# Tying a chunk's expert fetches to TensorE's late products, and the last keys' products by token halves

## The chip, the cores and the metric

The kernel runs on one core of one Trainium2 chip. The metric is the time of one execution in device microseconds (us), as the median of several runs. A profile is one further execution with the hardware profiler on, with a time of its own.

## The reference

It is one step of a one-layer decoder trunk (width 1024) on 512 prompt tokens and 32 sample tokens: retention heads beside a convolution module, then a retrieval of experts, each followed by a layer norm. The change lies wholly in the retrieval, which works on each token alone:

```python
idx = e1 * N_KEYS + e2                      # 8 heads x 16 experts of 128*128 per token
gate = softmax(sv)
u = take(peer_u, idx); act = gelu(einsum('phkd,pd->phk', u, xb))
vv = take(peer_v, idx); y = einsum('phk,phkd->pd', gate * act, vv)
x = layer_norm(ALPHA * x + y, ln2_g, ln2_b)
```

Every token has 128 slots (8 heads by 16 experts). An expert's row is 1024 numbers of `peer_u` and 1024 of `peer_v`, all in float32.

## The kernel before

**Two ways to do the same retrieval, side by side.** For 288 of the 544 tokens the kernel *gathers*: for one slot k, one indirect DMA on the GpSimd queue (a *fetch*, `gather`, line 587) brings 128 expert rows of 8 KB, one per token on its partition, 1 MiB in all. VectorE then multiplies the u half with the token and sums it (the *dot*, L590), ScalarE makes the weight from it (L598, L599), VectorE adds the weighted v half to the accumulator (L604). There are three chunks: 128 prompt tokens (indices `I0`, 128 slots), the 32 samples packed four heads side by side (`Is`, 32 slots), and 128 more prompt tokens (`Ib`, 128 slots; the diff tells this second chunk of 128 slots by `len(slots) == 128 and x1 is not x1_0`). The fetched tiles rotate: three buffers of `gp` and, for slots with k % 4 == 3, one of `gx2`. So fetch k starts when slot k-4 has been added up. The instructions of the queue of GpSimd stand in the order of the slots.

For the other 256 tokens the kernel does it *densely* on TensorE, over all 16,384 experts. Experts are taken in 128 groups, called keys here, of 128 experts each. For a key e two things are done, each with a row of 512 KB that SyncE loads into one of the four buffers of `uvp`:

- the *scores* (`scores_of`, L815): eight matmuls of 128x256; ScalarE's Gelu follows (`s_stage`, L915) and VectorE multiplies it with the gate weights (L918);
- the *products* (`v_row` loads, `v_products` multiplies, L924 and L930): for each half b of the tokens (128 each) two matmuls of 128x512 that add into two banks `pB[b][0]` and `pB[b][1]` of PSUM.

The profile shows a float32 matmul as two records, so a key's scores are 16 records and its products 8.

**Stages.** The gate weights of the keys come from one-hot products (`build`, L893 to L906): first those of keys 0 to 95 (`first_keys`), while keys 0 to 7 get their products for half 0 ahead of time. Then `phases` runs:

1. half 1 of keys 4 to 7, whose rows are still loaded, then half 1 of keys 0 to 3, whose rows are loaded again (L972);
2. keys 8 to 31 (L975);
3. keys 32 to 95 (L983). With each of the first sixteen goes a step of `last_keys`, which builds the weights of keys 96 to 127; with each of the next 32 (keys 48 to 79) goes the `s_stage` of one of the keys 96 to 127;
4. keys 96 to 123 (L991), then 124 to 127, written half by half in the text (L995).

`fetched` makes the gathered side: the norm of the first chunk, the sample chunk, its norm (`finish`, L607), then the chunk `Ib` and its norm. `run` interleaves both generators in the text, one step of `phases` and two of `fetched` by turns; the tile framework's scheduler then orders each engine's instructions by its own timeline, keeping data dependencies. `behind` (L166) adds an order without a semaphore. After both, the two halves of the dense tokens get their layer norm straight from the banks (L1024) and are written out.

Of the kernel before, what the change touches and what calls it, by code (L numbers as in the profile page):

```python
# [30 lines left out]
NG2 = NS + 128  # L31
ND = NR - NG2
TB = 8
KX = 48
UV = 4
AHEAD = 8
FREE = 20
EG = (32, 20, 44, 32)
E0S = (0, 32, 52, 96)

# [54 lines left out]
def tile_step(ctx: ExitStack, tc: tile.TileContext, a, o):  # L95
    nc = tc.nc
    V, S, T, G = nc.vector, nc.scalar, nc.tensor, nc.gpsimd
# [17 lines left out]
    def mmps():  # L115
        turn[0] += 1
        return banks[turn[0] % len(banks)].tile([128, 512], F32, name="mm")
# [352 lines left out]
    def residual(bank, xT, blocks, c0):  # L470

        for j, k in enumerate(blocks):
            T.matmul(bank[:, j * 128:(j + 1) * 128], xT[:, k, c0:c0 + 128], scaled, start=(j == 0), stop=False,
                     skip_group_check=True)

    def mix_mm(n, gT, y, c0, wo, xT=None):

        banks_ = [mmps(), mmps()]
        if xT is not None:
            for q in range(2):  # L480
                residual(banks_[q], xT, range(q * 4, q * 4 + 4), c0)
        for src, k0 in ((y, 4), (gT, 0)):
            for q in range(2):
                for s in range(2):
                    for k in range(4):
                        last = T.matmul(banks_[q][:n, s * 256:(s + 1) * 256], src[:, k, c0:c0 + n],  # L486
                                        wo[q * 2 + s][:, k0 + k, :], start=(xT is None and k0 == 4 and s == 0 and k == 0),
                                        stop=(k0 == 0 and s == 1 and k == 3), skip_group_check=True)
        return banks_, last
# [83 lines left out]
        V.reciprocal(sm[:n], sm[:n])  # L573
        V.tensor_mul(gate[:n, e0:e0 + nh], ex[:n], sm[:n].unsqueeze(2).to_broadcast([n, nh, TK]))

    gx2, fence, held = [], [], {}

    def hold(k, ins):

# [2 lines left out]
    def gather(x1, idx, gate, acc, slots):  # L582

        for k in slots:
            spare = gx if x1 is x1_0 and k < KX else (gx2[0] if gx2 and len(slots) == 128 else None)
            t = (spare if spare is not None and k % 4 == 3 else gp).tile([128, 2 * D], F32, name="g")
            G.indirect_dma_start(out=t, out_offset=None, in_=a["uv"],  # L587
                                 in_offset=bass.IndirectOffsetOnAxis(ap=idx[:, k:k + 1], axis=0))
            act = gw.tile([128, 2], F32, name="act")
            dot = V.scalar_tensor_tensor(t[:, :D], t[:, :D], 1.0, x1, op0=OP.mult, op1=OP.mult, accum_out=act[:, 0:1])  # L590
            if x1 is x1_0:
                for k0, ins in held.items():
                    if k >= k0:
                        behind(dot, ins)
            if fence and (len(slots) == 128 or k >= FREE):
                behind(dot, fence[0])
            wgt = gw.tile([128, 1], F32, name="wgt")
            S.activation(act[:, 1:2], act[:, 0:1], AF.Gelu)  # L598
            S.activation(wgt, act[:, 1:2], AF.Copy, scale=gate[:, k:k + 1])  # L599
            v = t[:, D:]  # L600
            if k == slots[0]:
                S.activation(acc, v, AF.Copy, scale=wgt)
            else:
                V.scalar_tensor_tensor(acc, v, wgt, acc, op0=OP.mult, op1=OP.add)  # L604
            yield
# [20 lines left out]
    x1_0 = per.tile([128, D], F32, name="x1_0")  # L626
# [16 lines left out]
    n = NR  # L643
# [34 lines left out]
    pm, last = mix_mm(128, g0, y0, 0, wo)  # L678
# [12 lines left out]
    x1T, xT = xT, xT[:, :, NS:]  # L691
# [103 lines left out]
    ln2 = [bc_row("lng", a["ln2_g"], D), bc_row("lnb", a["ln2_b"], D)]  # L795
    GW = {2: gap.tile([128, EG[2], ND], F32, name="Ga")}

    def place(e):

        g = max(i for i in range(4) if E0S[i] <= e)  # L800
        return GW[g][:, e - E0S[g]]

    def place2(e):

        g = max(i for i in range(4) if E0S[i] <= e)
        return GW[g][:, e - E0S[g]:e - E0S[g] + 2]

    def scores_of(e, ne=1):

        sp = pdn.tile([128, 2, ND], F32, name="sp")  # L810
        for i in range(ne):
            u = uvp.tile([128, D], F32, name="uv").rearrange("p (k e) -> p k e", k=8)
            nc.sync.dma_start(u, a["ut"][e + i])
            for k in range(8):
                T.matmul(sp[:, i], u[:, k], x1T[:, k, NG2:], start=(k == 0), stop=(k == 7), skip_group_check=True)  # L815
        return sp[:, 0:ne] if ne > 1 else sp[:, 0]

    qs = rp.tile([128, 16, n], F32, name="qs")
# [17 lines left out]
    for g in range(2):  # L836
# [9 lines left out]
        p = mmps().rearrange("p (q t) -> p q t", q=4)  # L846
# [16 lines left out]
    gb = gbs.enter_context(tc.tile_pool(name="gb", bufs=1, side="right", reuse_waits="tile"))  # L863
    GW[0] = gb.tile([128, EG[0], ND], F32, name="Gb")
    for e in range(0, EG[0], 2):
        S.activation(place2(e), scores_of(e, 2), AF.Gelu)
# [10 lines left out]
    for b in range(2):  # L877
        for q in range(2):
            residual(pB[b][q], x1T, range(q * 4, q * 4 + 4), NG2 + b * 128)
    GW[1] = gc.tile([128, EG[1], ND], F32, name="Gc")  # L880

# [26 lines left out]
                if t % nt == nt - 1:  # L908
                    yield pt, slice(t - nt + 1, t + 1), mm

    def s_stage(e, n=ND):

        sp, G_ = scores_of(e), place(e)
        W = dw_.tile([128, ND], F32, name="W")
        S.activation(W[:, :n], sp[:, :n], AF.Gelu)  # L915
        if n < ND:
            S.activation(G_[:, n:], sp[:, n:], AF.Gelu)
        V.tensor_mul(G_[:, :n], G_[:, :n], W[:, :n])  # L918

    ahead, marks = [], []  # L920

    def v_row(e):
        vt = uvp.tile([128, D], F32, name="uv")
        nc.sync.dma_start(vt, a["uv"][e * NK:(e + 1) * NK, D:])  # L924
        return vt

    def v_products(e, vt, b):
        W, ps_ = place(e), []
        for q in range(2):
            ps_.append(T.matmul(pB[b][q], W[:, b * 128:(b + 1) * 128], vt[:, q * 512:(q + 1) * 512],  # L930
                                start=False, stop=(e == NK - 1), skip_group_check=True))
        return ps_

    def first_keys():

        with tc.tile_pool(name="bt", bufs=2, reuse_waits="tile") as bt:
            done = 0
            for pt, ts, mm in build(bt, 0, E0S[3], 4):
                for g, e0, e1, ready in ((0, 0, EG[0], True), (2, 0, EG[2], True), (1, 0, done, True), (1, done, EG[1], False)):
                    if e0 == e1:  # L940
# [18 lines left out]
    def last_keys():  # L959

        with tc.tile_pool(name="bt", bufs=2, reuse_waits="tile") as bt:
            for pt, ts, _ in build(bt, E0S[3], EG[3], 16):
                S.activation(GW[3][:, :, ts], pt.rearrange("p t e -> p e t"), AF.Copy)
                yield

    def v_stage(e):
        vt = v_row(e)
        for b in range(2):
            v_products(e, vt, b)

    def phases():
        for e in [*range(AHEAD - UV, AHEAD), *range(AHEAD - UV)]:  # L972
            v_products(e, ahead[e] if e >= AHEAD - UV else v_row(e), 1)
            yield
        for e in range(len(ahead), EG[0]):  # L975
            v_stage(e)
            yield
        gbs.close()
        gd = ctx.enter_context(tc.tile_pool(name="gd", bufs=1, side="right", reuse_waits="tile"))
        GW[3] = gd.tile([128, EG[3], ND], F32, name="Gd")  # L980
        b = last_keys()
        more = iter(range(E0S[3], NK))
        for e in range(E0S[1], E0S[3]):  # L983
            v_stage(e)
            if next(b, "end") == "end":
                for _ in range(1):
                    k = next(more, None)
                    if k is not None:
                        s_stage(k)
            yield  # L990
        for e in range(E0S[3], NK - UV):  # L991
            v_stage(e)
            yield
        ends = [(e, v_row(e)) for e in range(NK - UV, NK)]
        for b in range(2):  # L995
            for e, vt in ends:
                v_products(e, vt, b)
                yield

    def fetched():  # L1000
# [21 lines left out]
    for b in range(2):  # L1022
        t = gp.tile([128, 2 * D], F32, name="g")[:, :D]
# [50 lines left out]
```

## Time and profile before

| | us |
|---|---|
| median of 3 runs (lowest, highest) | 1551.27 (1546.92, 1552.34) |
| the profiled execution's own time | 1557.44 |
| its span, first to last instruction | 1555.7 |
| TensorE busy | 1484.1 |
| VectorE busy | 1227.7 |
| ScalarE busy | 581.4 |
| GpSimd busy | 369.6 |

The mean granted TensorE clock of that execution was 0.983. Times inside the profile are counted from the start of its span. A row of the chain reads: start, duration, engine, tile and line, and how many records. A row of the timeline reads: start, duration, engine, line, operation, output and inputs, count, and in brackets the idle time of the engine just before it with what ended it. A row of the windows has, after the stretch and its length, the busy time of each engine with its number of records, then the granted clock (1.00 is full), the mean busy share of the 16 DMA engines, and the GB/s they moved.

### The profile page before, as it was taken

The page shows a single profiled execution, that of the slowest core. Times are in us where ns is not written, and L with a number is a line of the kernel's source. Part 1 is how long each engine was busy: PE and PEld are TensorE (multiplying, and loading weights), DVE is VectorE, ACT ScalarE, POOL GpSimd, SP SyncE. Part 2 cuts the span into 40 slices and gives each one's busy share as a digit, 9 for nine tenths or more (in the row PEclk, how much of TensorE's full clock was granted, in tenths as well). Part 3 has the DMA queues.
Part 4 walks back from the last instruction along what each step waited for, and adds up shares of the span by engine and source line. Part 5 has one row for each costly group of instructions (what it writes and reads, how often), then busy time and mean ns, then how long its engine had stood idle before and what let it go on. Part 6 is the DMA issues. An engine that isn't in the chain of part 4 may idle for free.

```text
span 1555.7 us, 20736 instructions
## 1 busy us (share of the span) xinstructions
PE 1484.1 (95%) x7046; PEld 1004.1 (65%) x7046; DVE 1227.7 (79%) x3151; ACT 581.4 (37%) x1633; POOL 369.6 (24%) x329
## 2 busy tenths in 40 slices
PE   6999999897999999999999999999999999999997
PEld 6978667565866668788888884444566555543333
DVE  4779998978747999999978988666777777766664
ACT  2224453125112333333534898426992111111110
POOL 2001225322312222312231101222223222322210
PEclk9999999998999999999999999999999999999999
DMA  9648787985688779999999624999999999999993
GB/s 362 243 153 353 252 297 257 347 334 206 226 339 341 273 260 363 358 330 346 366 382 360 240 88 177 394 350 402 347 372 394 423 424 424 424 424 424 424 410 121
DMA packets 100119, 505.85 MB, mean 325 GB/s; under 512 B 10247, under 2 KB 21255, under 8 KB 57125
## 3 DMA queue, kind: packets, MB, share of 16 engines
q0 software_dynamic: 42240, 305.12, 50.4%
q1 hardware_dynamic: 51325, 192.05, 32.4%
q10 hardware_dynamic: 6448, 7.36, 1.5%
q8 instruction: 55, 0.90, 0.2%
q14 instruction: 51, 0.42, 0.1%
HBM read 499.12 MB, written 5.80 MB: 325 GB/s over the span
## 4 chain that ended last, share of the span: by engine, by line
PE 55%; DVE 20%; DMA 12%; issue 9%; POOL 3%; ACT 2%; DVEq 0%; SPq 0%; POOLq 0%; ACTq 0%
PE pB L930 27%; PE sp L815 11%; DMA g<-in_uv_dram,I 6%; PE mm L199 5%; PE mm L486 5%; DVE acc L604 4%; DVE g L590 4%; PE mm L906 3%; POOL g L587 2%; DMA g<-in_uv_dram,Is 2%; DMA g<-in_w_in_dram 2%; DMA uv<-in_uv_dram 1%; PE mm L310 1%; DVE B L901 1%; DVE score L516 1%
## 5 line engine op out<-in xcount | busy, mean ns | idle before, releaser
L815 PE MATMUL sp<-x1T,uv 128*128 128x256 f32 x2048 | 464.1, 383 | 5.2 <-DMA uv<-in_ut_dram 2.8
L604 DVE SCALAR_TENSOR_TENSOR acc<-g,wgt,acc 128x1024 f32<-128x1024 f32 x285 | 364.5, 1279 | 102.0 <-ACT wgt L599 100.4
L815 PEld LDWEIGHTS sp<-x1T,uv 128*128 128x128 f32 x2048 | 384.7, 191 | 78.5 <-issue 28.2
L598 ACT ACTIVATE act<-act 128x1 f32<-128x1 f32 x288 | 57.8, 201 | 625.7 <-DVE g L590 625.4
L587 POOL DMA_INDIRECT g<-in_uv_dram,I x128 | 166.9, 1304 | 460.1 <-DVE acc L604 259.2
L590 DVE SCALAR_TENSOR_TENSOR g<-g,x1g 128x1024 f32<-128x1024 f32 x160 | 195.2, 1222 | 71.8 <-DMA g<-in_uv_dram,Ib 50.5
L587 POOL DMA_INDIRECT g<-in_uv_dram,Ib x128 | 140.6, 1098 | 442.0 <-DVE acc L604 293.7
L199 PE MATMUL mm<-x1T,w 128*128 128x384 f32 (+1 forms) x512 | 178.3, 504 | 1.5 <-ACT score L535 1.2
L590 DVE SCALAR_TENSOR_TENSOR g<-g,x 128x1024 f32<-128x1024 f32 x128 | 154.8, 1214 | 31.0 <-DMA g<-in_uv_dram,I 30.9
L930 PE MATMUL pB<-uv,Ga 128*128 128x512 f32 x352 | 162.1, 604 | 0.2
L893 ACT ACTIVATE off<-row,e1T 128x128 bf16<-128x128 bf16 x512 | 158.0, 388 | 1.0
L199 PEld LDWEIGHTS mm<-x1T,w 128*128 128x128 f32 x512 | 97.4, 192 | 73.7 <-issue 40.3
L930 PE MATMUL pB<-uv,Gb 128*128 128x512 f32 x256 | 113.5, 597 | 4.9 <-DMA uv<-in_uv_dram 4.5
L930 PEld LDWEIGHTS pB<-uv,Ga 128*128 128x128 f32 x352 | 63.7, 189 | 83.4 <-issue 63.1
L930 PE MATMUL pB<-uv,Gd 128*128 128x512 f32 x256 | 115.5, 599 | 0.8
L930 PEld LDWEIGHTS pB<-uv,Gd 128*128 128x128 f32 x256 | 46.7, 190 | 69.7 <-issue 69.5
L930 PEld LDWEIGHTS pB<-uv,Gb 128*128 128x128 f32 x256 | 47.4, 190 | 60.7 <-issue 52.9
L906 PEld LDWEIGHTS <-A 128*128 128x128 bf16 x1536 | 60.5, 96 | 31.3 <-issue 21.3
L901 DVE TENSOR_TENSOR B<-M,gtT 128x768 bf16<-128x768 bf16 (+1 forms) x192 | 69.4, 416 | 9.4 <-PE mm L906 9.2
L930 PE MATMUL pB<-uv,Gc 128*128 128x512 f32 x160 | 72.8, 600 | 0.0
L895 ACT ACTIVATE A<-off 128x1024 bf16<-128x1024 bf16 x64 | 67.4, 1053 | 9.3 <-PE mm L906 8.5
L906 PE MATMUL mm<-B,A 128*128 128x96 bf16 (+1 forms) x1536 | 63.9, 191 | 7.3 <-DVE Gc L947 6.5
(274 smaller groups left out, 1675.4 us busy)
## 6 DMA issues: line engine op xcount, KB each, us to landing
uv<-in_uv_dram SPq DMA_DIRECT2D x132, 512.0 KB
uv<-in_ut_dram SPq DMA_DIRECT2D x128, 512.0 KB
w<-in_w_in_dram SPq DMA_DIRECT2D x18, 1024.0 KB
w<-in_w_query_dram SPq DMA_DIRECT2D x16, 1024.0 KB
w<-in_w_out_dram SPq DMA_DIRECT2D x7, 1024.0 KB
g<-in_uv_dram,I POOLq DMA_INDIRECT x128
keys<-in_state_retention_dram ACTq DMA_DIRECT2D x4, 512.0 KB
out_dram<-keys SPq DMA_DIRECT2D x4, 512.0 KB
```

The costliest lines, as they stand in the source:

```text
L199: T.matmul(p[:, :n], w[m // 2][:, k, (m % 2) * 128:(m % 2 + 1) * 128], xT[:, k, c0:c0 + n], start=(k == 0), stop=(k == 7))
L486: last = T.matmul(banks_[q][:n, s * 256:(s + 1) * 256], src[:, k, c0:c0 + n], wo[q * 2 + s][:, k0 + k, :], start=(xT is None and k0 == 4 a ...
L587: G.indirect_dma_start(out=t, out_offset=None, in_=a["uv"], in_offset=bass.IndirectOffsetOnAxis(ap=idx[:, k:k + 1], axis=0))
L590: dot = V.scalar_tensor_tensor(t[:, :D], t[:, :D], 1.0, x1, op0=OP.mult, op1=OP.mult, accum_out=act[:, 0:1])
L598: S.activation(act[:, 1:2], act[:, 0:1], AF.Gelu)
L604: V.scalar_tensor_tensor(acc, v, wgt, acc, op0=OP.mult, op1=OP.add)
L815: T.matmul(sp[:, i], u[:, k], x1T[:, k, NG2:], start=(k == 0), stop=(k == 7), skip_group_check=True)
L893: S.activation(off[:, t], row, AF.Abs, bias=e1T[:, t1 + t:t1 + t + 1])
L895: S.activation(A, off, AF.Relu, bias=1.0, scale=-1.0)
L901: V.tensor_tensor(B[:, q], M, pairs_of(gtT[:, q], t1).to_broadcast([128, TB // 2, ne, 2]), op=OP.mult)
L906: mm = T.matmul(pt[:, t % nt], A[:, t - t1], B[:, q, (t - t1) // 2, :, t % 2], start=(q == 0), stop=(q == 2))
L930: ps_.append(T.matmul(pB[b][q], W[:, b * 128:(b + 1) * 128], vt[:, q * 512:(q + 1) * 512], start=False, stop=(e == NK - 1), skip_group_che ...
```

## The change

`PACE = (28, 15, 14)`. TensorE's late work is counted in *units*, a list to which matmuls are appended as the program's text comes by: the last matmul of every product pair of keys 48 to 123 and of every score of keys 96 to 127 (in the text: products 48, score 96, products 49, score 97 and so on to products 79, score 127, then products 80 to 123), and, of the last four keys, the last matmul of every second product of a half. That makes 64 + 44 + 4 = 112 units, 0 to 111. Fetch k of the chunk `Ib`, from slot 28 on, gets a semaphore dependency on unit (k - 28) * 15 // 14, so slot 28 waits for unit 0 and slot 127 for unit 106. In the text the generator yields until that unit exists. Fourteen fetches so go with fifteen units.

The first products of `phases` are regrouped: half 1 of keys 4 to 7 as before, then keys 8 to 31, and with keys 8 to 11 the half 1 of keys 0 to 3, one each.

The last four keys' products get an order among TensorE's instructions: those of half 1 stand behind the last one of half 0. In the kernel before, the scheduler had put them key by key, in spite of the text.

```diff
+PACE = (28, 15, 14)
...
+            unit = (k - PACE[0]) * PACE[1] // PACE[2] if len(slots) == 128 and x1 is not x1_0 else -1
+            while unit >= len(units):
+                yield
+            fetch = G.indirect_dma_start(out=t, out_offset=None, in_=a["uv"],
+                                         in_offset=bass.IndirectOffsetOnAxis(ap=idx[:, k:k + 1], axis=0))
+            if unit >= 0:
+                tc.add_manual_dep(fetch.ins, units[unit].ins.name, mybir.DependencyInfo(
+                    mybir.DependencyClass.Sync, mybir.DependencyReason.DATA), reason="pace")
...
-    def scores_of(e, ne=1):
+    def scores_of(e, ne=1, unit=False):
...
+                mm = T.matmul(sp[:, i], u[:, k], x1T[:, k, NG2:], start=(k == 0), stop=(k == 7), skip_group_check=True)
+        if unit:
+            units.append(mm)
...
     def v_stage(e):
         vt = v_row(e)
         for b in range(2):
-            v_products(e, vt, b)
+            ps_ = v_products(e, vt, b)
+        if e >= E0S[1] + ND // 16:
+            units.append(ps_[-1])
...
-        for e in [*range(AHEAD - UV, AHEAD), *range(AHEAD - UV)]:
-            v_products(e, ahead[e] if e >= AHEAD - UV else v_row(e), 1)
+        for e in range(AHEAD - UV, AHEAD):
+            v_products(e, ahead[e], 1)
             yield
-        for e in range(len(ahead), EG[0]):
+        for e in range(AHEAD, EG[0]):
             v_stage(e)
+            if e < 2 * AHEAD - UV:
+                v_products(e - AHEAD, v_row(e - AHEAD), 1)
             yield
...
-                        s_stage(k)
+                        s_stage(k, unit=True)
...
         for b in range(2):
             for e, vt in ends:
-                v_products(e, vt, b)
+                ps_ = v_products(e, vt, b)
+                if b:
+                    for p in ps_:
+                        behind(p, last)
+                else:
+                    last = ps_[-1]
+                if e % 2:
+                    units.append(ps_[-1])
                 yield
```

More of the change, by code (lines that the diff above doesn't have):

```diff
@@ L574, in retrieve @@
         V.tensor_mul(gate[:n, e0:e0 + nh], ex[:n], sm[:n].unsqueeze(2).to_broadcast([n, nh, TK]))
-    gx2, fence, held = [], [], {}
+    gx2, fence, held, units = [], [], {}, []
     def hold(k, ins):
@@ L586, in gather @@
             t = (spare if spare is not None and k % 4 == 3 else gp).tile([128, 2 * D], F32, name="g")
-            G.indirect_dma_start(out=t, out_offset=None, in_=a["uv"],
-                                 in_offset=bass.IndirectOffsetOnAxis(ap=idx[:, k:k + 1], axis=0))
+            unit = (k - PACE[0]) * PACE[1] // PACE[2] if len(slots) == 128 and x1 is not x1_0 else -1
[6 more added lines that the diff above has]
+                    mybir.DependencyClass.Sync, mybir.DependencyReason.DATA), reason="pace")
             act = gw.tile([128, 2], F32, name="act")
@@ L814, in scores_of @@
             for k in range(8):
-                T.matmul(sp[:, i], u[:, k], x1T[:, k, NG2:], start=(k == 0), stop=(k == 7), skip_group_check=True)
+                mm = T.matmul(sp[:, i], u[:, k], x1T[:, k, NG2:], start=(k == 0), stop=(k == 7), skip_group_check=True)
+        if unit:
+            units.append(mm)
         return sp[:, 0:ne] if ne > 1 else sp[:, 0]
@@ L909, in build, with s_stage @@
                     yield pt, slice(t - nt + 1, t + 1), mm
-    def s_stage(e, n=ND):
-        sp, G_ = scores_of(e), place(e)
+    def s_stage(e, n=ND, unit=False):
+        sp, G_ = scores_of(e, 1, unit), place(e)
         W = dw_.tile([128, ND], F32, name="W")
```

## The prediction

> **What bounds the kernel now.** I read the page's slices first, then the windows of the second half, then the chain.
>
> ```profile
> DMA  9648787985688779999999624999999999999993
> 1200.00:1280.00 80.00, 79.11 (x262) 47.70 (x261) 58.51 (x77) 14.78 (x54) 21.28 (x22) 1.00 1.02 424
> 1400.00:1500.00 100.00, 99.21 (x217) 38.81 (x216) 67.00 (x82) 13.44 (x54) 25.28 (x27) 1.00 1.02 424
> 1512.00:1518.00 6.00, 6.00 (x15) 2.48 (x14) 4.10 (x6) 0.62 (x3) 0.00 (x0) 1.00 0.80 301
> 1518.00:1535.00 17.00, 17.00 (x41) 7.50 (x40) 6.72 (x9) 1.95 (x4) 0.00 (x0) 1.00 0.56 186
> ```
>
> From 1200 to 1512 all 16 DMA engines are full (share 1.02, 424 GB/s). Then the fetches are over and the share falls to 0.80 and 0.56, while TensorE still has products to do.
>
> ```profile
> 983.50 79.08 PE pB L930 x184
> ...
> 1130.26 3.53 PE pB L930 x8
> 1134.38 3.55 PE sp L815 x16
> ...
> 1199.18 3.43 PE pB L930 x8
> 1202.62 3.69 PE sp L815 x16
> 1206.31 3.60 PE pB L930 x8
> ...
> 1511.59 33.10 PE pB L930 x76
> ```
>
> The chain runs on TensorE from 983 to 1544.69 (1511.59 + 33.10). A unit is 8 product records or 16 score records, one row of 512 KB. Unstretched, 184 records take 79.08, so a unit takes 8 x 0.43 = **3.44**. Unit 0 starts at 1130.26; scores are the odd units, and the piece at 1202.62 is the tenth of them from 1134.38 on, unit 19. So unit 18 ends at 1202.62. The 93 units from there end at 1544.69; the last 76 records are 9.5 of them, at 3.48. The other 83.5 take 1511.59 - 1202.62 = 308.97, **3.70** each: 0.26 above what TensorE needs.
>
> ```profile
> 1494.08 0.94 POOL L587 DMA_INDIRECT g<-in_uv_dram,Ib  x1 [2.79 <-DVE acc L604]
> 1497.79 0.94 POOL L587 DMA_INDIRECT g<-in_uv_dram,Ib  x1 [2.78 <-DVE acc L604]
> 1505.18 0.94 POOL L587 DMA_INDIRECT g<-in_uv_dram,Ib  x1 [2.75 <-DVE acc L604]
> 1516.61 1.23 DVE L590 SCALAR_TENSOR_TENSOR g<-g,x1g 128x1024 f32<-128x1024 f32 x1 [0.55 <-DMA g<-in_uv_dram,Ib]
> 1518.44 1.29 DVE L604 SCALAR_TENSOR_TENSOR acc<-g,wgt,acc 128x1024 f32<-128x1024 f32 x1 [0.60 <-ACT wgt L599]
> ```
>
> The fetches run at the same step, 3.71. One fetch (1.049 MB) and one row (0.524 MB) in 3.71 us is 1.573 / 3.71 = 0.424 MB per us, just the 424 of the windows. So DMA bounds this stage, TensorE waits 0.26 a unit for its rows, and the last fetch is issued at 1505.18, some 40 us before TensorE ends. It lands 11.43 later, with three others queued ahead of it.
>
> **The change part by part.** *The waits.* No byte and no matmul is added or removed; 100 fetches get one more semaphore.
>
> ```profile
> 1129.63 1.67 POOL L587 DMA_INDIRECT g<-in_uv_dram,Ib  x1 [2.08 <-DVE acc L604]
> ```
>
> This is the 29th fetch of the chunk, slot 28: it starts 4.2 before unit 0 ends (1130.26 + 3.53). At one fetch per unit the fetches now stay ahead; with 14 in 15 units each waits in its turn, more and more of them. A unit's share of DMA is then 0.524 + 14/15 x 1.049 = 1.503 MB; at the 424 GB/s of the windows that takes **3.545**. Bounds: 3.44 below, where TensorE itself is the limit, and 3.683 above, if a unit with a fetch still takes 3.70 and only the fifteenth 3.44. I take 3.545, since the share is 1.02 and TensorE has four row buffers to carry a gain of one unit into the next.
>
> From unit 19 to unit 106 are 88 units: 1202.62 + 88 x 3.545 = **1514.6** for the end of unit 106, at which the last fetch starts (before, unit 106 ended at 1544.69 - 5 x 3.48 = 1527.3).
>
> The Trainium skill, "DMA: Bandwidth & Descriptors", section "Where 436 GB/s comes from", puts transfers from HBM to SBUF at about 358 GB/s; by it a unit would take 4.20 after and 4.39 before, and the windows' 424 speak against it.
>
> Behind a waiting fetch GpSimd has only later fetches. But VectorE and ScalarE work in order too: behind a fetch's dot and its Gelu stand, in the changed order, the one-hot blocks of the last keys that TensorE needs inside units 3 to 9. The tightest: ScalarE's last block stands behind the Gelu of slot 33, which waits for unit 5; TensorE wants it in the middle of unit 9, 3.6 units or about 13 us later. How long a fetch takes on an empty queue the trace shows once, after the pause for the samples' norm (below the window that shows ScalarE full, 39.77 of 40, where those blocks are made):
>
> ```profile
> 1120.00:1160.00 40.00, 40.00 (x324) 25.59 (x323) 29.04 (x64) 39.77 (x118) 11.71 (x9) 1.00 0.97 368
> 1028.29 1.18 POOL L587 DMA_INDIRECT g<-in_uv_dram,Ib  x1 [5.16 <-ACT act L598]
> 1036.45 1.23 DVE L590 SCALAR_TENSOR_TENSOR g<-g,x1g 128x1024 f32<-128x1024 f32 x1 [2.77 <-DMA g<-in_uv_dram,Ib]
> ```
>
> From issue to dot **8.2**; with a full queue 11.4 (above). Dot, Gelu and block add under 3. So 13 is enough at 8.2, and about 1 short at 11.4. A paced fetch meets one other at most: I take 8.2 and cost nothing; the other end is 4 block pairs x 1.
>
> *The last four keys by halves.* Their rows are needed 1.72 apart rather than 3.44. Three rows and a fetch outstanding at unit 106 and one more row at unit 107 are 3.1 MB, 7.4 us at 424 GB/s; the last is wanted 3.44 + 3 x 1.72 = 8.6 after unit 106. Bounds 0 and 5.2 (rows still 3.44 apart); I take 1.0, near the low end. TensorE then ends at 1514.6 + 5 x 3.44 + 1.0 = **1532.8**, 11.9 earlier.
>
> *The tail.* VectorE is in order, and the changed order puts the norm of the gathered chunk in among those of the banks.
>
> ```profile
> 1519.76 1.29 DVE L611 SCALAR_TENSOR_TENSOR yt<-x1g,acc 128x512 f32<-128x512 f32 x2
> 1520.97 1.28 DVE L452 BATCH_NORM_STATS2 lst<-yt 128x6 f32<-128x512 f32 x2
> 1522.53 1.28 DVE L461 SCALAR_TENSOR_TENSOR yt<-yt,lmv,lng 128x1024 f32<-128x1024 f32 x1
> 1524.39 1.28 DVE L466 SCALAR_TENSOR_TENSOR yt<-yt,lrs,lnb 128x1024 f32<-128x1024 f32 x1
> 1544.71 0.70 DVE L452 BATCH_NORM_STATS2 lst<-pB 128x6 f32<-128x512 f32 x1 [0.16 <-PE pB L930]
> 1545.44 0.21 DVE L453 BATCH_NORM_AGGREGATE lmv<-lst 128x2 f32<-128x12 f32 x1
> 1546.18 1.39 DVE L461 SCALAR_TENSOR_TENSOR g<-pB,lmv,lng 128x512 f32<-128x512 f32 x2
> 1551.04 0.15 DVE L464 RECIPROCAL lrs<-lrs 128x1 f32<-128x1 f32 x1
> 1551.22 1.41 DVE L466 SCALAR_TENSOR_TENSOR g<-g,lrs,lnb 128x512 f32<-128x512 f32 x2
> ```
>
> From the last fetch: 8.2 to its dot, 3.1 to the end of its addition (1516.61 to 1519.73), then all the norms in one row: 1.29 + 1.28 + 1.28 + 1.28 for the chunk, per half 1.3 + 0.2 + 1.4 + 0.15 + 1.4, and 0.2 for the chunk's aggregate, 14.2 with its reciprocal, about 14.1 as neighbours overlap. That is 1514.6 + 25.4 = **1540.0**. From TensorE's end: stats 0.7, the chunk's 1.28, half 0's 1.40, stats 0.7, then 0.2 + 1.4 + 0.15 + 1.4 for half 1, less 0.4 as the first stats need not await the last matmul: 1532.8 + 6.8 = 1539.6. The later holds. Before, VectorE ended at 1551.22 + 1.41 = 1552.63 and the span 3.07 later; the output writes stay. So the span becomes 1543.1, **12.6** less than 1555.7.
>
> *The regrouped first products.*
>
> ```profile
> 960.00:1000.00 40.00, 35.51 (x172) 16.55 (x171) 25.95 (x51) 23.25 (x71) 9.38 (x10) 1.00 0.96 371
> 967.00 1.98 PE L930 MATMUL pB<-uv,Gb 128*128 128x512 f32 x4 [1.80 <-DMA uv<-in_uv_dram]
> 971.81 1.98 PE L930 MATMUL pB<-uv,Gb 128*128 128x512 f32 x4 [0.64 <-DMA uv<-in_uv_dram]
> 975.48 1.99 PE L930 MATMUL pB<-uv,Gb 128*128 128x512 f32 x4 [0.97 <-DMA uv<-in_uv_dram]
> 979.21 3.70 PE L930 MATMUL pB<-uv,Gb 128*128 128x512 f32 x8 [1.08 <-DMA uv<-in_uv_dram]
> ```
>
> Here TensorE waits 4.5 in all for rows. The change spreads four half-used rows over four fully used ones, but the same rows have to come and DMA is 0.96 full; and a one-hot block of VectorE now stands behind one fetch more, some 3 to 5 us of possible wait. Between a gain of 4.5 and a loss of 5 I take 0.
>
> **Sum.** The profiled execution would go from 1557.44 to 1544.8. It lies 6.2 above the median shown; the same 12.6 off 1551.27 gives **1539**. About 0.5% (7.8 us) is what a measurement of this kernel can tell from no change: faster means under 1543.5, slower above 1559.
>
> **The rivals.** *Locked to the fetch (0.11).* Rows and fetches go one to one now, 3.70 and 3.71. If that is a turn by turn between the two queues, a unit with a fetch stays 3.70 and the gain is only the fifteenth: 88 x 3.683 puts unit 106 at 1526.7, the span at 1526.7 + 25.4 + 3.07 = 1555.2: **1551**. The Trainium skill, same page, section "Queues, rings and completion order", says that each DMA engine takes turns between its queues, a packet at a time; the equal steps agree. Against it: row buffers fill in the fetchless unit and lend to the next ones.
>
> *The waits never bind (0.05).* If slots stay behind their units, nothing happens: **1551**. Against it: the 4.2 by which slot 28 is early, and 1505.18 for the last.
>
> *TensorE's floor (0.08).* If DMA has more to give, units take 3.44: 88 x 3.44 = 302.7, and with the 4.5 of the first products unit 106 ends at 1500.8, the span at 1529.3, 26.4 less: **1525**. Against it: the share of 1.02 at 424.
>
> *Blocks stuck behind waiting fetches (0.12).* The place is units 3 to 9, where the order leaves 13 us from a unit to the block that stands behind its fetch. From about 10.5 us of landing on, each microsecond more stops TensorE in four block pairs, and paced units hold back the fetches in turn. At 17 it costs 4 x 6.5 = 26 on top of the 12.6 won: **1565**, slower; from 16 it shows. For it: 11.4 with a full queue, and ScalarE full where it happens. Against: 8.2 on an empty one.
>
> **How the numbers follow.** The forecast, 1533 to 1543, gets 0.64; it takes in the row wait and the landing. Faster is 0.64 + 0.08 = 0.72, the same 0.11 + 0.05 = 0.16, slower 0.12. With 0.64 the range must reach the cases at 1551 as well (0.80) and a little of the one below: 1530 to 1553.
>
> **What would show it.** After about 1200: fetch steps of 3.8 rather than 3.71, GpSimd's idle time ended by TensorE, units of 3.55, share still about 1.0, and the fall of the share only in the last 15 us. The last fetch near 1515, issue to dot 8 to 9. In the last 16 product records, half 0's norm work beside half 1. I would be wrong if units stayed at 3.70 with the DMA share below 1, if waits of TensorE for VectorE or ScalarE turned up between 1130 and 1180, or if the last fetch's norm ended over 3 us after 1540.

## The result and the profile after

The changed kernel takes 1551.16 us (median of 22 runs, 1537.03 to 1560.53) beside 1560.04 for the kernel before (22 runs on the same chips, 1546.92 to 1567.5). The ratio is 0.9947, 95% interval 0.9924 to 0.9969: it is faster by 8.3 us, with an interval of 4.8 to 11.9 (the two medians alone lie 8.9 apart). The forecast was 12.6 us off, a ratio of 0.9919, which lies just outside. Two further sets of runs of the same kernel gave 0.9941 (0.9922 to 0.996) and 0.9945 (0.9918 to 0.9972). The forecast time of 1539 missed by 12.2 us, mostly because its base, the median of three runs, was 8.8 below that of 22.

The profiled execution of after took 1559.73 with a span of 1558.0, more than the 1557.44 and 1555.7 of before. The reason shows ahead of the paced part. These two rows are unit 0 (the product behind a batch of small matmuls) and unit 19 in the timeline of TensorE, after:

```profile
1137.77 3.68 PE L939 MATMUL pB<-uv,Gc 128*128 128x512 f32 x8
...
1209.79 3.62 PE L822 MATMUL sp<-x1T,uv 128*128 128x256 f32 x16
```

Unit 0 starts at 1137.77 rather than at 1130.26, and unit 19 at 1209.79 rather than at 1202.62. The 7 us were there before any wait could act. Another profile of the very same kernel starts unit 0 at 1142.88, and one of the variants below at 1126.55, with the same work ahead of it:

```profile
1142.88 3.68 PE L939 MATMUL pB<-uv,Gc 128*128 128x512 f32 x8
```

```profile
1126.55 3.68 PE L939 MATMUL pB<-uv,Gc 128*128 128x512 f32 x8
```

The scatter stands ahead of the regrouped part already: in the profiles of this document the first product of half 1 starts anywhere from 953.5 to 971.2. The granted clock goes some of the way with it (0.97 up to unit 0 in the profile that starts it at 1142.88, 0.98 in the one at 1126.55). So single spans are of no use here for an effect of 8 us. What can be compared is the stretch from unit 0 to VectorE's last instruction: 1552.63 - 1130.26 = 422.4 before. After, the last fetches, and what VectorE does with the last one, are these rows of the timelines of GpSimd and VectorE:

```profile
1517.83 0.94 POOL L591 DMA_INDIRECT g<-in_uv_dram,Ib  x1 [2.78 <-PE pB L939]
1525.21 0.94 POOL L591 DMA_INDIRECT g<-in_uv_dram,Ib  x1 [6.44 <-PE pB L939]
1528.94 0.94 POOL L591 DMA_INDIRECT g<-in_uv_dram,Ib  x1 [2.79 <-PE pB L939]
```

```profile
1538.15 1.23 DVE L597 SCALAR_TENSOR_TENSOR g<-g,x1g 128x1024 f32<-128x1024 f32 x1 [1.84 <-DMA g<-in_uv_dram,Ib]
...
1539.99 1.28 DVE L611 SCALAR_TENSOR_TENSOR acc<-g,wgt,acc 128x1024 f32<-128x1024 f32 x1 [0.60 <-ACT wgt L606]
1541.31 1.29 DVE L618 SCALAR_TENSOR_TENSOR yt<-x1g,acc 128x512 f32<-128x512 f32 x2
...
1553.51 1.41 DVE L467 SCALAR_TENSOR_TENSOR g<-g,lrs,lnb 128x512 f32<-128x512 f32 x2
```

The fetches now stop for TensorE (the releaser in the brackets is a product, L939, where before it was VectorE's addition), one unit is skipped between 1517.83 and 1525.21, and the last fetch starts at 1528.94 rather than 1505.18. VectorE ends at 1554.92, so the stretch is 417.2, 5.2 less than before; in the two further profiles of the change it is 413.4 and 413.3. The mean, 7.8 less, is what the times say.

DMA works longer, until the last fetch has landed at about 1538: the windows of after, with the DMA share and the GB/s as the last two columns:

```profile
1200.00:1280.00 80.00, 79.54 (x271) 50.53 (x270) 55.02 (x73) 13.43 (x52) 23.95 (x22) 1.00 1.01 418
1400.00:1500.00 100.00, 99.46 (x221) 40.08 (x220) 65.22 (x79) 12.93 (x52) 37.28 (x26) 1.00 1.01 417
1512.00:1518.00 6.00, 5.92 (x14) 2.27 (x13) 3.81 (x6) 0.99 (x4) 1.10 (x2) 1.00 1.02 423
1518.00:1535.00 17.00, 16.94 (x40) 7.05 (x38) 10.01 (x12) 1.99 (x8) 2.64 (x3) 1.00 0.99 384
```

From 1518 to 1535 the share is 0.99 instead of 0.56: the emptiness of the old tail is filled. But from 1200 to 1500 it moves 417 to 418 GB/s, not 424. The chain of after (start, duration, engine, tile and line, records), and its first line of shares:

```profile
PE 40%; DVE 24%; DMA 18%; issue 10%; ACT 4%; POOL 3%; SPq 0%; POOLq 0%; DVEq 0%; ACTq 0%
```

```profile
1367.24 11.79 DMA uv<-in_uv_dram
...
1419.77 17.45 PE pB L939 x40
1437.47 11.55 DMA g<-in_uv_dram,Ib
1449.21 11.02 DMA g<-in_uv_dram,Ib
...
1528.94 9.19 DMA g<-in_uv_dram,Ib
```

Before, the chain ran on TensorE from 983 to the end. Now it passes between row loads, TensorE (40 records in 17.45, 3.49 a unit) and fetches, and its end is the last fetch and VectorE's norms behind it, where before TensorE's products led up to the norms.

### The profile page after: what moved, and what is told of

The parts are those of the page before. It is cut to its first block, busy times and chain, and to the rows that moved or that the text cites. A ratio compares the mean times of both kernels' runs of the same rounds, so it can differ in the third digit from the quotient of the medians.

```text
span 1558.0 us, 20737 instructions
## 1 busy us (share of the span) xinstructions
PE 1479.0 (95%) x7046; PEld 1006.9 (65%) x7046; DVE 1226.4 (79%) x3151; ACT 579.5 (37%) x1633; POOL 390.4 (25%) x329
## 4 chain that ended last, share of the span: by engine, by line
PE 40%; DVE 24%; DMA 18%; issue 10%; ACT 4%; POOL 3%; SPq 0%; POOLq 0%; DVEq 0%; ACTq 0%
PE sp L822 13%; PE pB L939 13%; DMA g<-in_uv_dram,Ib 7%; DVE acc L611 6%; PE mm L487 5%; DMA g<-in_uv_dram,I 5%; DVE g L597 4%; PE mm L200 4%; POOL g L591 3%; PE mm L915 2%; DMA uv<-in_ut_dram 2%; DMA g<-in_w_in_dram 2%; ACT off L902 1%; DMA uv<-in_uv_dram 1%; DVE B L910 1%
## 5 line engine op out<-in xcount | busy, mean ns | idle before, releaser
L591 POOL DMA_INDIRECT g<-in_uv_dram,I x128 | 170.7, 1333 | 461.6 <-DVE acc L611 257.9
L591 POOL DMA_INDIRECT g<-in_uv_dram,Ib x128 | 158.7, 1240 | 443.7 <-DVE acc L611 127.7
L939 PE MATMUL pB<-uv,Ga 128*128 128x512 f32 x352 | 159.9, 599 | 1.8 <-DMA uv<-in_uv_dram 1.7
L939 PE MATMUL pB<-uv,Gd 128*128 128x512 f32 x256 | 115.2, 598 | 2.3 <-DMA uv<-in_uv_dram 1.6
L939 PEld LDWEIGHTS pB<-uv,Ga 128*128 128x128 f32 x352 | 65.0, 190 | 80.5 <-issue 64.1
L939 PE MATMUL pB<-uv,Gb 128*128 128x512 f32 x256 | 113.5, 597 | 2.4 <-DMA uv<-in_uv_dram 1.9
L939 PEld LDWEIGHTS pB<-uv,Gd 128*128 128x128 f32 x256 | 46.7, 190 | 70.6 <-issue 62.7
L939 PEld LDWEIGHTS pB<-uv,Gb 128*128 128x128 f32 x256 | 47.3, 190 | 58.0 <-issue 53.0
L939 PE MATMUL pB<-uv,Gc 128*128 128x512 f32 x160 | 72.7, 600 | 0.0
```

The lines of the kernel that those rows point to most:

```text
L591: fetch = G.indirect_dma_start(out=t, out_offset=None, in_=a["uv"], in_offset=bass.IndirectOffsetOnAxis(ap=idx[:, k:k + 1], axis=0))
```

## The experiments

My theory: the whole gain is the spreading of the fetches over more units, and it fell short because units did not get down to 3.545 and the last fetch then sets the end. Rivals: the regrouped first products or the order by halves win or lose something; the waits win by a shorter fetch queue and not by spreading; TensorE, not the fetch, sets the end. All ratios are against the kernel before, run beside the variant on the same chip.

| kernel | ratio (95%) | unit, mean of 18 to 105 | last fetch, from the end of unit 106 | unit 0 to VectorE's end |
|---|---|---|---|---|
| before | 1 | 3.711 | -24.0 | 422.4 |
| the change (three sets) | 0.9947, 0.9941, 0.9945 | 3.621, 3.581, 3.577 | +0.3 | 417.2, 413.4, 413.3 |
| e1 waits only | 0.9943 (0.9913 to 0.9972) | 3.591 | +0.3 | 414.7 |
| e2 all but the waits | 0.9986 (0.9962 to 1.0009) | 3.705 | -29.1 | 421.4 |
| e3 waits and halves | 0.994 (0.991 to 0.997) | 3.603 | +0.3 | 415.5 |
| e4 nine fetches in ten units | 0.9996 (0.9976 to 1.0016) | 3.494 | +18.0 | 419.6 |
| e9 a fetch per unit | 0.9975 (0.9953 to 0.9997) | 3.695 | -21.8 | 418.8 |
| e12 from slot 31 | 0.9941 (0.9921 to 0.9961) | 3.609 | -13.2 | 411.6 |
| e13 from slot 35 | 0.9983 (0.9957 to 1.0009) | 3.697 | -27.1 | 419.9 |
| e5, e17 cap at unit 101 | 0.991 (0.9883 to 0.9938), 0.9951 (0.9931 to 0.9971) | 3.586, 3.571 | -4.0, -2.7 | 412.0, 411.9 |
| e16 cap at 104 | 0.9954 (0.993 to 0.9977) | 3.580 | -4.2 | 411.3 |
| e18 cap at 97 | 0.9948 (0.9928 to 0.9968) | 3.572 | -3.9 | 410.8 |
| e15 waits only, cap at 101 | 0.9968 (0.9945 to 0.999) | 3.586 | -4.5 | 414.2 |
| e10 without the chunk's norm | 0.9916 (0.9889 to 0.9944) | 3.578 | +0.3 | 410.0 |

The last three columns are read from the records of each profile: starts of units 18 and 106, a difference over 88; the last indirect DMA's start; VectorE's last record. (For before, unit 0 is taken where the chain enters it, 0.15 us behind its record.)

**One part alone.** e1 keeps the waits and takes the other two edits back, e3 takes back only the regrouped first products (the first part of the diff), and e2 takes back the waits alone, by a condition that no slot meets:

```diff
-        for e in range(AHEAD - UV, AHEAD):
-            v_products(e, ahead[e], 1)
+        for e in [*range(AHEAD - UV, AHEAD), *range(AHEAD - UV)]:
+            v_products(e, ahead[e] if e >= AHEAD - UV else v_row(e), 1)
...
-                if b:
-                    for p in ps_:
-                        behind(p, last)
```

```diff
-            unit = (k - PACE[0]) * PACE[1] // PACE[2] if len(slots) == 128 and x1 is not x1_0 else -1
+            unit = (k - PACE[0]) * PACE[1] // PACE[2] if False else -1
```

> Only the waits: the order of the first products and that of the last four keys as before. My theory (the spreading of the fetches is the whole gain): the same ratio as the change, about 0.995, units 18 to 106 at 3.62 against 3.71 before, some 8 us less. Rival 'the regrouped first products cost': clearly better than the change, 0.992 or less. Rival 'the halves matter at the end': worse than the change by 2 to 5 us, because the last four rows are then needed by half 0 and half 1 in the old order and the fetch tail stands behind.

> The waits are left out; the regrouped first products and the last keys' new order stay. My theory: no change from the kernel before, 0.998 to 1.002, units back at 3.70 and all fetches over some 35 us before TensorE ends. Rival 'the regroup costs' (in the profile after, 1.0 us came from that stage): 1.001 to 1.004. Rival 'the regroup or the halves are what wins': 0.996 or less.

> Waits and the last keys' new order; the first products as before. My theory: as the change, 0.995, since the regroup is worth between -1 and +1 us. Rival 'the regroup costs': 0.992 or less, and the stretch from the first dense product to key 48 shorter than the change's by several us.

All three came as my theory had it. With the waits alone the ratio is 0.9943; with the waits taken out 0.9986, with an interval that holds 1, and the windows and the chain of e2 are those of before:

```profile
1400.00:1500.00 100.00, 99.08 (x217) 38.67 (x216) 67.96 (x82) 13.43 (x54) 25.36 (x27) 1.00 1.02 424
```

```profile
1494.49 7.34 PE pB L939 x16
1509.32 38.24 PE pB L939 x88
```

Two units take 7.34, 3.67 each, until the fetches are over; then eleven take 38.24, 3.48 each. e3 says that the first products are worth nothing measurable, and the profiles agree: from the first product of half 1 to unit 0 the fourteen with the regrouping take 171.0 to 173.8 us, the four without it 171.9 to 173.4, both 172.3 in the mean. The waits are the cause of the gain: only with them do the units fall from 3.71 to about 3.6.

**Spreading, or a shorter queue?** e9 keeps the waits with one fetch per unit, e4 spreads further, with (28, 10, 9) in the same place:

```diff
-PACE = (28, 15, 14)
+PACE = (28, 1, 1)
```

> One fetch per unit: slot 28 still waits for unit 0, slot 127 for unit 99. The wait is there and the fetches cannot run ahead, but the ratio of fetches to units is that of the kernel before. My theory (only the spreading over more units helps): units at 3.70, unit 18 to 106 at 3.68 to 3.72, ratio 0.998 to 1.002. Rival 'it is the shorter fetch queue that lets rows through': units below 3.62 and a ratio of 0.995.

> Nine fetches in ten units instead of fourteen in fifteen; the last fetch then waits for unit 110 instead of 106. My theory (every skipped fetch frees about nine units to TensorE's floor of 3.44, and the last fetch with the norms behind it sets the end): units near 3.50 to 3.55, so unit 106 some 6 to 9 us earlier than in the change, but the last fetch starts four units (14 us) later in the count, so the span comes out 4 to 8 us longer than the change's, ratio 0.998 to 1.000. Rival 'TensorE's end sets the time': 5 to 8 us faster than the change, 0.990. Rival 'a unit with a fetch is locked at 3.70 whatever the ratio': units 3.67, time some 15 us above the change.

In e9 the units stay at 3.695 and DMA at 424 in the window:

```profile
1400.00:1500.00 100.00, 99.36 (x218) 39.02 (x217) 67.50 (x82) 13.43 (x54) 49.10 (x27) 1.00 1.02 424
```

Its ratio of 0.9975 is a little below what I had put down, but the units are where they were: a wait without fewer fetches per unit shortens nothing there. What its stretch gains, 3.6 us, is mostly the tail: from the end of unit 106 to VectorE's end it takes 21.1 in e9 as in e2, 23.4 before; that is the order by halves. (In e9 only 13 of the 100 fetches start within 0.5 us of their unit's end; the others come up to 3.6 us later, held by DMA's own step of 3.7.) In e4 the units go down to 3.494, the shortest of all, so the spreading is what shortens them. And the time came back all the same. The last fetch in the chain of e4, and VectorE's last record:

```profile
1536.51 5.70 DMA g<-in_uv_dram,Ib
```

```profile
1555.78 2.73 DVE L467 SCALAR_TENSOR_TENSOR g<-g,lrs,lnb 128x512 f32<-128x512 f32 x4
```

The last fetch waits for unit 110 and starts at 1536.51, 18 us after unit 106. Even at 5.70 for the landing, what follows it ends at 1558.51. That is the price of pacing: each unit that the last fetch is put off moves it and all the norms behind it. The forecast for e4, 0.998 to 1.000, held.

**TensorE's own pace.** e11 leaves the fetches of slots 28 to 127 out:

```diff
+            if unit >= 0:
+                yield
+                continue
             fetch = G.indirect_dma_start(out=t, out_offset=None, in_=a["uv"],
```

> Leaves out slots 28 to 127 of the second chunk altogether: their fetches, dots and additions, so that only TensorE's rows are loaded there. Both theories want TensorE's own pace from it: units of 3.44, 303 us from unit 18 to unit 106, about 152 GB/s. If rows alone do not bring the units below 3.5, part of what I put down to the fetches is something else.

One execution took 1534.55. Its chain and one window:

```profile
1361.00 164.81 PE pB L942 x384
```

```profile
1300.00:1400.00 100.00, 100.00 (x306) 57.91 (x305) 3.83 (x9) 3.45 (x9) 0.00 (x0) 1.00 0.47 153
```

384 records in 164.81 are 48 units at 3.43, TensorE's floor. What is above it in the other kernels comes with the fetches; that TensorE then waits for rows, and not for VectorE's work on what was fetched, fits e1 below, where 14 units run at 3.46 with a fetch and its dot for each. And there is something unforeseen in the last two columns: rows alone take 0.47 of the engines' time for 153 GB/s, that is 326 GB/s for a full share, where rows and fetches together reach 424 at 1.02, or 416.

**Why the units did not reach 3.545.** In e1 series of short and of long units follow each other. Its chain and its windows:

```profile
1408.51 48.38 PE pB L939 x112
1464.34 14.18 PE pB L939 x32
1478.54 7.34 PE pB L939 x16
```

```profile
1410.00:1450.00 40.00, 40.00 (x95) 17.68 (x94) 25.63 (x31) 4.98 (x20) 14.90 (x12) 1.00 1.02 418
1465.00:1515.00 50.00, 49.72 (x112) 19.83 (x110) 33.24 (x40) 6.46 (x26) 14.34 (x13) 1.00 1.02 425
```

Behind a skipped fetch 14 units run at 48.38 / 14 = 3.46; behind the next one only three or four do (14.18 for four), and then pairs take 7.34 again, 3.67 each. Over the short units DMA moves 418, over the mostly long ones 425. Four windows of 4 us show one place where it falls, and below them stand the packets of the two queues (q1 has the rows, q0 the fetches; each with packets, MB and its share of the 16 engines' time) from 1227 to 1228:

```profile
1218.00:1222.00 4.00, 4.00 (x17) 2.97 (x16) 2.63 (x5) 0.77 (x3) 1.19 (x1) 1.00 1.02 411
1222.00:1226.00 4.00, 4.00 (x16) 2.57 (x15) 3.40 (x5) 0.50 (x2) 1.19 (x1) 1.00 1.02 425
1226.00:1230.00 4.00, 4.00 (x14) 2.43 (x13) 2.99 (x5) 0.77 (x3) 1.19 (x1) 1.00 0.99 354
1230.00:1234.00 4.00, 4.00 (x18) 3.11 (x17) 3.40 (x5) 0.50 (x2) 1.61 (x2) 1.00 1.01 422
```

```profile
DMA packets 73, 0.28 MB, mean 283 GB/s; under 512 B 10, under 2 KB 10, under 8 KB 67
q1 hardware_dynamic: 63, 0.23, 77.7%
q0 software_dynamic: 10, 0.05, 11.8%
```

From 1226 to 1230 the engines are nearly as busy as ever and move 354; within it, from 1227 to 1228, the rows' queue is nearly alone and 283 GB/s go with a share of 0.90, or 316 for a full one, near the 326 of e11. The packets of the whole stretch say that this is the rule: cut from unit 18 to unit 100 into steps of 1 us, the kernel before has 4% of steps in which the rows' queue takes more than half of the packets' time, the three profiles of the change 12 to 15%. In those steps DMA moves 396 to 404 GB/s in the change; in the steps where the fetches take 50 to 90% of the time it moves 421 to 424, and 424 before. Some 60 to 99% of what the change lacks to 424 falls into those steps (53 to 77% if the steps are made 2 us long, and 36% in e3, so they are not all of it). They are spread over all fifteen units, and not only behind the skipped fetch. Whether the waits leave too little outstanding was tried by counting the slots from a later one, which lets every fetch start some three (e12, the diff) or seven (e13, with 35 for 31) units earlier:

```diff
-PACE = (28, 15, 14)
+PACE = (31, 15, 14)
```

> Fourteen fetches per fifteen units as in the change, but counted from slot 31: every fetch waits for a unit three (here and there four) earlier, the last one for unit 102. What is open is why the paced kernels moved 418 to 421 GB/s from unit 18 to 106 instead of 424. Theory A (a fetch that is bound to the unit just ended leaves DMA too little to do, and three units of slack give it back): units of 3.55 to 3.56, and with the earlier last fetch a ratio of 0.988 to 0.990. Theory B (the paced mixture itself costs it, however loose the wait): units of 3.58 to 3.60, and only the tail is shorter, ratio 0.990 to 0.992 as with the cap. Rival C (so loose a wait binds no more): units above 3.65, ratio 0.995 or more.

> As the last, counted from slot 35: seven or eight units looser, the last fetch waits for unit 98. If the wait still binds in the second half, units lie between 3.55 and 3.65 and TensorE's end sets the time, ratio 0.991 to 0.994: slower than counting from slot 31, because the fetches now end some 10 us before TensorE does and DMA has nothing but rows there. Rival 'earlier is always better for the tail': 0.989 or less.

In e12, theory A fell: 3.609 a unit, and the window moves 421, not 424. (Its waits bind only from about slot 59 on; from unit 48 to unit 106, where they do, a unit takes 3.580 and DMA moves 421 as well.)

```profile
1400.00:1500.00 100.00, 99.67 (x226) 41.36 (x225) 65.93 (x79) 13.05 (x53) 34.67 (x27) 1.00 1.02 421
```

Theory B named the unit nearly (3.58 to 3.60) and missed the ratio, 0.9941 for 0.990 to 0.992. The change itself, in the same set of runs, gave 0.9941 too, where I had expected it some 5 us above its variants with an earlier last fetch. In e13 I was wrong altogether: the wait does not bind any more, and the units are those of before.

```profile
1400.00:1500.00 100.00, 99.04 (x217) 38.81 (x216) 67.99 (x82) 13.43 (x54) 48.93 (x27) 1.00 1.02 424
```

So the gain depends on waits that bind, seven units of slack undo it, and with them comes a DMA rate of 417 to 422. It is lower mostly in the moments when the fetches' queue has run thin; why it runs thin even with three units of slack stays open, and no run took these moments away.

**The end.** If the last fetch sets the end, to bring it forward or to leave out the norm behind it must pay. e5 and e17 cap the unit for which a fetch waits at 101 (e16 at 104, e18 at 97), e15 does so with the waits alone, e10 writes the accumulator of the second chunk without its norm:

```diff
+            unit = min(unit, 101)
...
-            finish(x1g, [ac[:, 0:512], ac[:, 512:]], w_, [(0, w_, dst)], t, g == "b")
+            if g == "b":
+                nc.sync.dma_start(dst, ac)
+            else:
+                finish(x1g, [ac[:, 0:512], ac[:, 512:]], w_, [(0, w_, dst)], t, g == "b")
```

> Leaves out the norm of the second chunk's gathered tokens (their accumulator is written out as it is). My theory (VectorE's norms, one after the other behind the last fetch, end the span): 2 to 4 us below the change, after which TensorE's last products set the end. Rival 'the end is TensorE's already': at most 1.3 us below, the one instruction of that norm that stands ahead of the last stats.

> The change, but no fetch waits for a unit after 101, so slots 123 to 127 may start one behind the other from there on. My theory (the last fetch and VectorE's norms behind it end the span, with TensorE's end some 3 us earlier than needed): the last fetch starts 2 to 4 us earlier against unit 106, and the time comes 1 to 3 us below the change, ratio 0.992 to 0.994. Rival 'TensorE's end sets the time': 0 to 1 us above the change, since the last units get a fetch each and lengthen.

> Only the waits, none later than unit 101; first products and last keys in the order of before. My theory (the waits and the place of the last fetch are everything): 0.990 to 0.993, as the cap with the whole change. Rival 'once TensorE's end sets the time the order by halves pays', because half 0's norm can run beside half 1's products: 3 to 5 us worse than the cap with the whole change, 0.994.

e10's ratio of 0.9916 is 4 to 5 us below the change's, at the upper edge of what was expected or over it (the intervals touch), and its stretch in the profile is 3.3 us shorter than in the change's two further profiles. The time alone does not show it, as the change was not in that set of runs and another kernel of the set, e5, came out lower there than when it was repeated. The row of VectorE in which the last addition ends, and its last one:

```profile
1525.37 1.28 DVE L611 SCALAR_TENSOR_TENSOR acc<-g,wgt,acc 128x1024 f32<-128x1024 f32 x1 [0.60 <-ACT wgt L606]
...
1533.24 0.70 DVE L453 BATCH_NORM_STATS2 lst<-pB 128x6 f32<-128x512 f32 x1 [1.75 <-PE pB L939]
...
1536.60 1.41 DVE L467 SCALAR_TENSOR_TENSOR g<-g,lrs,lnb 128x512 f32<-128x512 f32 x2
```

Without the chunk's norm VectorE waits for TensorE again (1.75 ahead of the stats). So in the change, by the profile, it is VectorE with the chunk's norm behind the last fetch that sets the end. The first cap, e5, came out at 0.991, better than anything else, but in another set than the change. The two were then run side by side, with a later and an earlier cap:

> The cap at unit 101 again, now beside the change. If the place of the last fetch costs the change time: 2 to 5 us below the change. If it was chance: within 1.5 us of it.

> The change, beside the caps: 0.994 to 0.995, as in both sets before.

> No fetch waits for a unit after 104: only the last three go earlier. Tail theory: between the change and the cap at 101, 1 to 3 us below the change. Rival 'the tail does not matter': as the change.

> No fetch waits for a unit after 97: nine or ten go as fast as their buffers allow. Tail theory with TensorE's end as the next bound: no better than the cap at 101, 0 to 3 us above it, because the last units get a full fetch each again (3.70) while the norms already wait for TensorE. Rival 'the earlier the last fetch the better': 2 us or more below the cap at 101.

Side by side the ratios are 0.9951, 0.9945, 0.9954 and 0.9948: no difference that the intervals can tell. The 0.991 of six runs did not come again, and no variant is shown to beat the change. In the profiles the caps shorten the stretch by 1.3 to 2.5 us against the change's 413.3, too little for these times. VectorE's last record and the last fetch at a cap of 104 show why it is no more:

```profile
1511.34 0.94 POOL L592 DMA_INDIRECT g<-in_uv_dram,Ib  x1 [1.34 <-DVE acc L612]
```

```profile
1538.06 1.42 DVE L467 SCALAR_TENSOR_TENSOR g<-g,lrs,lnb 128x512 f32<-128x512 f32 x2
```

The fetch starts 4.4 us earlier against unit 106 than in the change, but behind others; it needs 11.4 to its dot instead of 8.4 to 9.2, and TensorE's last products stand close behind. e15 missed its expectation of 0.990 to 0.993 and went the rival's way, past its 0.994 (its interval still overlaps e17's, so the time does not show it). The profile shows what the rival meant: without the order by halves VectorE has nothing to do while the last products run.

```profile
1539.46 0.70 DVE L453 BATCH_NORM_STATS2 lst<-pB 128x6 f32<-128x512 f32 x1 [2.43 <-PE pB L940]
...
1547.38 2.74 DVE L467 SCALAR_TENSOR_TENSOR g<-g,lrs,lnb 128x512 f32<-128x512 f32 x4
```

All four bank norms (x4 in the last row) come behind TensorE's end. In e2, where only the order by halves is left at the end, VectorE ends 3.9 after TensorE's last record, and before 6.3; that 2.3 us is in the profile, and the time of e2 (-2.2 us, interval -5.9 to +1.4) agrees without showing it. In the change itself the halves win nothing, as the fetch ends later than TensorE.

## Why the prediction was right or wrong, point by point

| term | forecast | after, profiled | its two further profiles |
|---|---|---|---|
| end of unit 18 | 1202.62 | 1209.79 | no matter |
| unit, from there to unit 106 | 3.545 | 3.62 | 3.58, 3.58 |
| last fetch, issue to dot | 8.2 | 9.2 | 8.4, 8.6 |
| end of unit 106 to VectorE's end | 25.4 | 26.3 | 25.4, 26.3 |
| from there to the span's end | 3.07 | 3.08 | |

- **What bounds the kernel: right.** DMA was the bound, its emptiness in the last 15 to 40 us was the reserve, and spreading the fetches uses it (e1, e2, e4, e9). e11 shows the floor of 3.43 that I had put at 3.44.
- **"A unit's share of DMA ... takes 3.545": the step that failed.** The bytes were right; the 424 GB/s by which I divided them were not. The units of the change took 3.59 in the mean of three profiles, 1.503 / 3.593 = 0.418 MB per us, and in all twelve profiles in which fourteen fetches in fifteen units were held 3.57 to 3.62. Per unit that is 0.048 more than forecast, over 88 units 4.2 us, nearly all that the 12.6 lacked. I took 424 for what a full share of the engines moves. It holds where both queues have work, as they always had before; in the change the rows' queue has most of the time in 12 to 15% of the steps, and DMA moves 396 to 404 GB/s there. Most of the shortfall lies there, by the packets; no run shows that it would go if those steps were filled, and the rest is not explained. Some of the longer units are single ones in which TensorE waits long for a row; the profile after has two of them (first fence) and that of before one (second):

```profile
1281.98 2.18 PE L822 MATMUL sp<-x1T,uv 128*128 128x256 f32 x9 [1.17 <-DMA uv<-in_ut_dram]
...
1379.07 6.49 PE L939 MATMUL pB<-uv,Ga 128*128 128x512 f32 x14 [1.45 <-DMA uv<-in_uv_dram]
```

```profile
1300.56 3.69 PE L815 MATMUL sp<-x1T,uv 128*128 128x256 f32 x16 [1.63 <-DMA uv<-in_ut_dram]
```

- **The tail from the last fetch: right** (8.2 against 8.4 to 9.2, 25.4 against 25.4 to 26.3), 0.6 us in the mean. I had also said that an end of the last norm over 3 us after 1540 would prove me wrong: it ended at 1554.92, of which 7.2 us are the late start and 6.9 the units.
- **The end of TensorE before: misread, without harm to the sum.** I took the last row of the chain, 1544.69, for TensorE's end. The timeline of before says otherwise:

```profile
1519.62 26.77 PE L930 MATMUL pB<-uv,Gd 128*128 128x512 f32 x62
```

  Its end is 1546.39; at 1544.69 only half 0's banks let VectorE go. So unit 106 ended at 1529.2, not 1527.3, and VectorE 23.4 later. Against that the change's tail of 26 costs 2.6 us that I had booked as nothing, and the units had 2 us more to win. As the sum was made to the span's end, both errors cancel.
- **The last four keys' rows, 1.0 (bounds 0 to 5.2): right in place, too small in size.** From the end of unit 106 TensorE takes 1.6 to 2.9 us more than five units of 3.44 in the three profiles of the change. After, it waits 1.63 for one of the rows, and that is hidden, as the fetch ends later:

```profile
1538.88 8.82 PE L939 MATMUL pB<-uv,Gd 128*128 128x512 f32 x20 [1.63 <-DMA uv<-in_uv_dram]
```

- **The regrouped first products at 0: right**, by the ratios of e1 and e3 within their intervals, and by the 172.3 us with and without them.
- **The blocks behind paced fetches at 0: right.** From unit 0 to unit 18 it takes 68.6 to 69.1 us in the three profiles of the change and 68.9 in that of before. The tightest fetch, slot 33, took 9.0 us from issue to dot in all three, more than the 8.2 that I took and less than the 10.5 from which it would have cost. So the rival that would have made the kernel slower did not come about.
- **"Locked to the fetch": wrong as a rule, half true in the picture.** The 14 units of e1 at 3.46, most of them with a fetch each, show that a fetch does not cost a unit 0.26. But the fetchless unit's credit is used up after three to fourteen units, and the rest run at 3.67 to 3.70. The Trainium skill, "DMA: Bandwidth & Descriptors", section "Queues, rings and completion order", has each engine take turns between its queues by packets; that shares the engines, and e1 shows that it does not tie a row to a fetch.
- **"The waits never bind": wrong.** After, slot 28 starts 0.3 us behind the end of unit 0 and the later ones at most 2.9 behind theirs. Counted from seven slots later, as in e13, it would have been right.
- **"TensorE's floor": wrong**, though e4 comes to 3.494 with a tail that takes it back.

What stays open: why the fetches' queue runs thin under the waits, what else keeps DMA at 417 to 422 GB/s rather than 424, and how much of the 4 us is single late rows.

## What to carry to other kernels

Where DMA is the bound and falls idle before the end, transfers that are not urgent can be put off so that the urgent ones come faster; but what is gained per unit has to be set against the work that stands behind the last one put off, and both have to be worked out to the end of the span (e4 won 19 us in the units and lost nearly all of it behind the last fetch). A wait is worth something only while it binds: counting from seven slots later took the gain away. And where the same code's start scatters by 16 us from run to run, compare stretches from a mark inside the profile, and repeat a variant that looks best: 0.991 became 0.995.

## What the runs showed of the hardware that was not expected

- The busy share of the DMA engines is not a measure of bytes: 0.47 went with 153 GB/s where rows ran alone (e11), 1.02 with 424 where rows and fetches ran together, and in one stretch of 4 us 0.99 with 354 (e1).
- A fetch of 1 MiB took 5.7 us from issue to its dot where the rows were over (e4), 8.1 to 9.2 with rows beside it and one or two fetches not yet used (e1, the change), 11.4 with three queued ahead (before, and the caps).
- A single row can come late, 1.17 and 1.45 us after and 1.63 before, with nothing beside it in these views that explains it.
